# FoX attention values: block transposes on VectorE and fp32 products on eight 32x64 array tiles, with the values replicated through DRAM

## The chip, the cores and the metric

The kernel runs on one core of a Trainium2 chip. A core has TensorE (matrix products; the profile shows its products as PE and its weight loads as PEld), VectorE (DVE), ScalarE (ACT), GpSimd (POOL) and SyncE (SP), which here issues nearly all DMAs. Operands lie in SBUF, products arrive in PSUM (eight banks of 512 fp32 columns on 128 partitions). The metric is the device time of one execution in microseconds, as a median over runs. A profile comes from one execution of its own.

## The reference

One decoder layer for 1024 tokens of width 1024. An RMS norm and one input projection feed two groups of heads: eight HGRN2 heads (a gated linear recurrence) and sixteen FoX heads (softmax attention with a cumulative forget gate). Their gated outputs go through an output projection, a per-layer embedding gate and a final norm. What matters here is the FoX part, for a head of 64 features:

```python
for blk in range(S // Q):                      # Q = 128 queries
    q0, q1 = blk * Q, (blk + 1) * Q
    logits = einsum('bhtd,bhsd->bhts', qb, kb) * scale + F[..., q0:q1, None] - F[..., None, :q1]
    probs = softmax(where(mask, logits, -inf), axis=-1)
    outs.append(einsum('bhts,bhsd->bhtd', probs, vb))
```

So a block of 128 queries sees all earlier keys, and within its own 128 keys a triangle. All is fp32.

## The kernel before

The work goes in four stages: the start (norm, embeddings), the HGRN heads, the FoX heads, and the output projection with the gate and the final norm. Everything is kept feature-major, and fp32 accuracy is reached in the dense products by splitting both operands into exact float32r parts, hi and lo: three products (L363 in the helper `product_steps`) make one. A dense column tile (128 output features, 1024 tokens) is 48 such products of 512 columns.

The dense projections are not a stage of their own. The class `Ahead` holds them as jobs, generators that issue one product per step, and `ahead.fill(columns)` puts about so many columns of dense work between the steps of the heads. The tables `HGRN_FILL` and `FOX_FILL` give the amounts; `ahead.until(mark)` forces jobs until a tile is done; `ahead.flush()` issues what was put off in `ahead.pending`. `ahead.weights()` hands over a weight tile and starts the load of the next, in the order listed in `w_in_loads`. TensorE's instructions are pinned to program order by `pe`; the other engines follow the order that the scheduler finds.

The sixteen FoX heads go in eight pairs p (a pair fills 128 partitions), head i of a pair, and two chunks c of 512 queries, c = 1 first. A `Chunk` runs:

- `biases` and `diagonals`: loads the head's cumulative gate for all partitions, and GpSimd adds the causal bias for the four diagonal blocks.
- `softmax(b)` for a block of 128 queries, n = 128 (b + 1) keys: logits on TensorE in one or two pieces of up to 512 columns (L816 with the hi part of the keys, L817 with the lo part), on VectorE a fused add and minimum per piece (L820) and the minimum over the pieces (L826), on ScalarE the exponential with its sum (L827). The queries lie on the partitions.
- `transposed(j)`: TensorE transposes the 128x128 blocks of keys j for the chunk's query blocks (L835), ScalarE rounds the result out of PSUM into the float32r hi part (L844), VectorE subtracts for the lo part (L845). For the last key block of a chunk only half of a 256-column tile is live; its other half is zero (`last`, L838 and L839).
- `mix(following)`: over the key blocks j of the chunk, the two products of values with the hi and lo parts of the probabilities (L867, L868), accumulated in one PSUM bank. A value tile holds hi and lo of V side by side in its 128 columns, so the two halves of the result are added at the end (L873, L874). Between them go the softmaxes of the following chunk and the dense fills, and after j = 3 the flush.
- `norms`: the reciprocal of the softmax sums, transposed and passed through DRAM (`zd`, L887 and L888).

`fox_v(p)` makes the values: a dense tile, evacuated as `vt` (L480), transposed by four TensorE transposes per half (L485), and split into hi and lo in `vs` (L490, L491). PSUM in this stage: two banks for dense products, three for logits (`lg`), two for transposes (`tr`), one for the output (`av`).

In a pair, the jobs of the next pair are appended in the order q, k, gate of this pair (only pairs 1 to 5), v. The last chunk of a pair is preceded by `ahead.until(("k", p + 1))`. At the end, eight y tiles of the HGRN half are read back (`y_load`) into buffers of the FoX stage as these come free, four before pair 7 and four before the last chunk.

Of the kernel before, what the change touches and what calls it, by code (L numbers as in the profile page):

```python
# [33 lines left out]
FOX_FILL = (  # L34
    (1660, 3670, 8820, 2130, 2400),
    (3650, 8080, 7350, 2840, 3200),
    (3650, 8080, 7350, 2840, 3200),
    (3650, 8080, 7350, 2840, 3200),
    (3650, 8080, 7350, 2840, 3200),
    (3650, 8080, 7350, 2840, 3200),  # L40
    (2320, 5140, 6980, 2420, 2720),
    (1830, 4040, 7350, 1280, 1440),
)

# column tiles of w_in (128 columns each)
# [3 lines left out]
def shape_constants():  # L49
    """Identity, causal bias and block masks: functions of the shapes alone."""  # L50
# [3 lines left out]
    # keys (rows, within blocks of 32) that the columns of a block's three score groups keep  # L54
# [15 lines left out]
def trunk(ctx: ExitStack, tc: tile.TileContext, a, out):  # L70
# [12 lines left out]
    zd = dram.tile([16, S], F32, name="zd")  # L83

# [5 lines left out]
    def load_w(src, k, lo_engine=None, pin=lambda ins: ins):  # L90
        """One 128-column weight tile as exact float32r parts [P, k, P]."""
# [7 lines left out]
    def product(ps, terms, pin=lambda ins: ins):  # L99
        """ps = sum over terms of (stationary hi, lo) x (moving hi, lo), lo x lo left to rounding."""  # L100
# [6 lines left out]
    def dense(src, mov, evac, k=KT, lo_engine=None, w=None):  # L107
        """Feature-major projection of one column tile: evac(chunk, psum [P, CH])."""
# [7 lines left out]
    def add_squares(acc, sq, with_eps=False, pin=lambda ins: ins):  # L116
        """acc += sq; EPS enters the sum over the partitions once, so that ps / D below is mean + EPS."""
# [5 lines left out]
    def rstd(y, t, ps, pin=lambda ins: ins):  # L123
        """y = (ps / D) ** -0.5: the table's value and one Newton step."""
# [11 lines left out]
    def load_pair(tile0):  # L136
        """Two column tiles of w_in side by side, [P, k, 256], as float32r parts."""
# [8 lines left out]
    def token_major(w, v, blocks, evac_pin=lambda ins: ins):  # L146
        """Two column tiles with the tokens on partitions, [P, 2, block, 128]."""
# [6 lines left out]
    with ExitStack() as st:  # L154
# [3 lines left out]
        pin = tc.keep_in_program_order  # this section's engines run in the order below  # L158
# [36 lines left out]
        # per-layer embedding (halved), a [128, 512] piece at a time  # L195
# [118 lines left out]
        # HGRN lower bound: softmax over the single layer, cumulative sum minus the first  # L314
# [11 lines left out]
    class Ahead:  # L326
        """Dense products that fill the tensor engine's waits; weights are loaded a tile ahead."""
# [19 lines left out]
        def fill(self, columns=None):  # L347
            """Run jobs for about so many columns of moving operands, or all of them."""
# [27 lines left out]
    def w_in_loads():  # L376
# [4 lines left out]
        for p in range(PAIRS_F - 1):  # L381
            tiles += [T_FQ + p + 1, T_FK + p + 1] + ([T_FG + p] if 0 < p < PAIRS_F - 2 else []) + [T_FV + p + 1]
# [385 lines left out]
    with fox as st:  # L768
# [7 lines left out]
        for i in range(2):  # L776
            t = [fp.tile([P, 2 * P], F32R, name=f"last{i}{j}", bufs=1) for j in range(2)]
            for x in t:
                zeros(x[:, :P])
            last.append(t)  # L780

        class Chunk:
# [65 lines left out]
            def mix(self, following):  # L848
# [9 lines left out]
                for j in range(nj):  # L858
                    ph, pl, c0 = nxt
                    if j + 1 < nj:  # L860
                        nxt = self.transposed(j + 1)
# [265 lines left out]
```

## Time and profile before

| | |
|---|---|
| median of 3 runs | 1362.83 us (1361.51 to 1363.41) |
| span of the profiled execution, first to last instruction | 1361.6 us |
| mean granted TensorE clock | 0.993 |
| instructions | 22260 |
| FoX stage, from the first probability transpose to the last product with values | 563.9 to 1082 us |
| HBM read, written | 82.59 MB, 16.91 MB |

The profile names instructions by line, engine, operation and tiles, output left of the arrow. A group's line gives its count, then its busy time in us and the mean duration of one in ns, then the idle time of its engine just before it and what ended that. Durations of TensorE products overlap: a product's record lasts until its modelled end, while the next has long begun, so the distance between starts is what one costs in a stream. In the timeline a row starts with its start time and duration in us; consecutive instructions of one kind are merged, with a count. A row of the table by stage gives the stretch, its length, then busy us and instruction count for PE, PEld, DVE, ACT and POOL, then the granted clock (1.00 is full), the DMA engines' share and GB/s.

### The profile page before, as it was taken

To read this page: it belongs to the slowest core of one execution; us is meant where nothing else is said; L and a number is where in the kernel's file an instruction comes from. 1 tells how busy PE (TensorE), PEld (TensorE's weight loads), DVE (VectorE), ACT (ScalarE), POOL (GpSimd) and SP (SyncE) were. 2 spreads that over 40 slices of the span, in tenths; PEclk is the share of its full clock that TensorE was granted. 3 is DMA by queue.
4 is the path that set the end of the run, shared out by engine and by line. 5 is a ranking of instruction groups with operands and counts; after the bars stand their busy time and mean duration, and the time that the engine had idled before them with its cause. 6 is when DMAs were issued, how large, how long until landed. Compare 5 with 4: busy or idle time off the path is not lost.

```text
span 1361.6 us, 22260 instructions
## 1 busy us (share of the span) xinstructions
PE 1324.1 (97%) x8756; PEld 1116.9 (82%) x8756; DVE 802.6 (59%) x1976; ACT 552.6 (41%) x1128; POOL 373.7 (27%) x352
## 2 busy tenths in 40 slices
PE   6899999999999999999999999999999999999996
PEld 4787888888888878888888888888888888888895
DVE  6746575656746576576566666666666843333465
ACT  5413122221312233565555555555565711222455
POOL 3613123112211122344333333333342210101232
PEclk9999999999999999999999999999999999999998
DMA  7411111101101012112121112111123163212312
GB/s 282 144 45 63 48 38 58 63 17 63 48 32 63 19 47 80 47 56 70 55 71 55 56 55 70 54 55 55 70 84 118 63 240 108 85 47 70 132 63 78
DMA packets 35080, 100.93 MB, mean 74 GB/s; under 512 B 5008, under 2 KB 7312, under 8 KB 34976
## 3 DMA queue, kind: packets, MB, share of 16 engines
q1 hardware_dynamic: 34832, 98.99, 20.8%
q8 instruction: 69, 1.13, 0.3%
q0 software_dynamic: 144, 0.52, 0.1%
q14 instruction: 35, 0.29, 0.1%
HBM read 82.59 MB, written 16.91 MB: 73 GB/s over the span
## 4 chain that ended last, share of the span: by engine, by line
PE 87%; DVE 7%; ACT 4%; issue 1%; DMA 1%; SPq 0%; POOL 0%; DVEq 0%; ACTq 0%; POOLq 0%
PE ps L363 47%; PE pt L835 5%; PE ps L105 5%; PE ps L103 5%; PE ps L104 4%; PE po L868 3%; PE po L867 3%; PE lg L816 2%; PE lg L817 2%; PE ps L569 1%; PE gps L105 1%; PE gps L104 1%; PE gps L103 1%; DVE x L279 1%; PE po L712 1%
## 5 line engine op out<-in xcount | busy, mean ns | idle before, releaser
L363 PE MATMUL ps<-uhi,whi 128*128 128x512 f32 x896 | 355.9, 397 | 0.3 <-DVE q L451 0.3
L363 PE MATMUL ps<-ulo,whi 128*128 128x512 f32 x896 | 355.5, 397 | 0.0
L363 PE MATMUL ps<-uhi,wlo 128*128 128x512 f32 x896 | 354.6, 396 | 0.0
L88 POOL TENSOR_TENSOR wlo<-wf,whi 128x1024 fp32r<-128x1024 f32 x59 | 145.3, 2463 | 377.4 <-ACT whi L87 370.8
L363 PEld LDWEIGHTS ps<-uhi,whi 128*128 128x128 f32 x896 | 168.4, 188 | 31.5 <-PE ps L363 0.7
L363 PEld LDWEIGHTS ps<-ulo,whi 128*128 128x128 f32 x896 | 168.5, 188 | 30.4
L363 PEld LDWEIGHTS ps<-uhi,wlo 128*128 128x128 f32 x896 | 168.5, 188 | 30.4
L87 ACT CAST whi<-wf 128x1024 fp32r<-128x1024 f32 (+1 forms) x77 | 79.8, 1038 | 168.7 <-PE ps L104 90.4
L827 ACT ACTIVATE pr<-pr,mx 128x1024 f32<-128x1024 f32 (+7 forms) x128 | 99.6, 778 | 101.3 <-DVE mx L826 94.8
L845 DVE TENSOR_TENSOR pl<-pt,ph 128x512 fp32r<-128x512 f32 (+2 forms) x160 | 94.7, 607 | 75.9 <-ACT ph L844 74.6
L801 POOL TENSOR_TENSOR fm<-fbc,cst 128x128 f32<-128x128 f32 x128 | 59.0, 462 | 251.1 <-DVE mx L826 129.4
L844 ACT CAST ph<-pt 128x512 fp32r<-128x512 f32 (+2 forms) x160 | 79.8, 520 | 70.7 <-PE pt L835 60.1
L105 PE MATMUL ps<-yhi,wlo 128*128 128x512 f32 x256 | 99.6, 389 | 0.0
L103 PE MATMUL ps<-yhi,whi 128*128 128x512 f32 x256 | 99.6, 389 | 0.0
L104 PE MATMUL ps<-ylo,whi 128*128 128x512 f32 x256 | 99.6, 389 | 0.0
L820 DVE CUSTOM_DVE_ANT_0 pr<-lg,fbc 128x512 f32<-128x512 f32 (+3 forms) x176 | 82.0, 490 | 15.5 <-PE lg L817 15.2
L835 PE MATMUL pt<-cst,pr 128*128 128x128 f32 x576 | 89.3, 272 | 1.1 <-ACT pr L827 0.9
L835 PEld LDWEIGHTS pt<-cst,pr 128*128 128x128 f32 x576 | 71.4, 140 | 19.6 <-ACT pr L827 2.2
L816 PE MATMUL lg<-kh,q 128*128 128x512 f32 x192 | 74.7, 389 | 0.0
L817 PE MATMUL lg<-kl,q 128*128 128x512 f32 x192 | 64.1, 341 | 0.0
L867 PE MATMUL po<-ph,vs 128*128 128x512 f32 (+2 forms) x160 | 57.8, 361 | 0.1
L868 PE MATMUL po<-pl,vs 128*128 128x512 f32 (+2 forms) x160 | 57.9, 362 | 0.0
(214 smaller groups left out, 2498.3 us busy)
## 6 DMA issues: line engine op xcount, KB each, us to landing
wf<-in_w_in_dram SPq DMA_DIRECT2D x64, 512.0 KB
fbc<-fd SPq DMA_DIRECT2D x16, 512.0 KB
yf<-yd SPq DMA_DIRECT2D x16, 512.0 KB
wf<-in_w_out_dram SPq DMA_DIRECT2D x16, 512.0 KB
x<-in_xT_dram SPq DMA_DIRECT2D x8, 512.0 KB
pled<-pleo SPq DMA_DIRECT2D x16, 256.0 KB
xr<-in_xT_dram SPq DMA_DIRECT2D x16, 256.0 KB
yd<-sg SPq DMA_DIRECT2D x8, 512.0 KB
```

What stands on the lines that cost most here:

```text
L88: pin(lo_engine.tensor_tensor(out=lo, in0=src, in1=hi, op=ALU.subtract))
L103: pin(mm(ps, whi, uhi, start=i == 0, stop=False))
L104: pin(mm(ps, whi, ulo, start=False, stop=False))
L105: pin(mm(ps, wlo, uhi, start=False, stop=i == n - 1))
L363: pe(mm(ps, x, y, start=i == j == 0, stop=i == n - 1 and j == 2))
L816: pe(mm(ps[:, :w], tq, kh[:, s0 : s0 + w], start=True, stop=False))
L817: pe(mm(ps[:, :w], tq, kl[:, s0 : s0 + w], start=False, stop=True))
L827: nc.scalar.activation(pr, pr, AF.Exp, bias=mx[:, 0:1], scale=-1.0, accum_out=zs[:, b : b + 1])
L835: pe(nc.tensor.transpose(pt[:, b * P : (b + 1) * P], self.probs[b][:, j * P : (j + 1) * P], ident))
L845: nc.vector.tensor_tensor(out=pl, in0=pt[:, c0:], in1=ph, op=ALU.subtract)
L867: pe(mm(po[:, c0:], vs[:, j], ph, start=j == 0, stop=False))
L868: pe(mm(po[:, c0:], vs[:, j], pl, start=False, stop=j == nj - 1))
```

## The change

The probabilities are no longer transposed on TensorE. After the exponential, VectorE transposes the whole block row in one instruction, in blocks of 32x32: within each group of 32 partitions (queries 32 a to 32 a + 31 of the block) the result has keys on the partitions and queries along the free axis. The product with the values then contracts over 32 keys at a time, in fp32 without a split, on tiles of 32 rows and 64 columns of the array: row group a belongs to the queries 32 a, and even and odd key groups s go to the two column halves, with one PSUM bank per row group. Since row group a needs the values of key group s on its own 32 partitions, the values are needed on all four groups of partitions. They are written to DRAM and read back four times.

```diff
-    (3650, 8080, 7350, 2840, 3200),
+    (6500, 6500, 3300, 5700),
...
-            tiles += [T_FQ + p + 1, T_FK + p + 1] + ([T_FG + p] if 0 < p < PAIRS_F - 2 else []) + [T_FV + p + 1]
+            tiles += [T_FV + p + 1, T_FQ + p + 1, T_FK + p + 1] + ([T_FG + p] if 0 < p < PAIRS_F - 2 else [])
...
-                pt = tr.tile([P, CH], F32, name="pt", tag="tr")
+                pt = lg.tile([P, CH], F32, name="pt", tag="lg")
...
-                    nc.scalar.copy(dst[:, :, hi], pv[:, :, hi])
-                    nc.vector.tensor_tensor(out=dst[:, :, lo], in0=pv[:, :, hi], in1=dst[:, :, hi], op=ALU.subtract)
+                vo = fp.tile([P, 4, P], F32, name="vo", tag="tmp", bufs=3)
+                nc.scalar.copy(vo.rearrange("p b d -> p (b d)"), pt)
+                nc.sync.dma_start(out=vd[p, c * CH : (c + 1) * CH, :].rearrange("(b t) d -> t b d", t=P), in_=vo)
...
+    def load_v(p, quarters):
+        for g in quarters:
+            t = v_t.setdefault(p, [None] * 4)[g] = fp.tile([P, 8, P], F32, name=f"vr{g}", bufs=1)
+            for i in range(4):
+                nc.sync.dma_start(
+                    out=t[32 * i : 32 * i + 32], in_=vd[p, 256 * g : 256 * g + 256, :].rearrange("(s k) d -> k s d", k=32)
+                )
...
-        lg = st.enter_context(tc.tile_pool(name="lg", bufs=3, space=PSUM, reuse_waits="tile"))
-        tr = st.enter_context(tc.tile_pool(name="tr", bufs=2, space=PSUM, reuse_waits="tile"))
+        lg = st.enter_context(tc.tile_pool(name="lg", bufs=2, space=PSUM, reuse_waits="tile"))
...
-                self.probs[b - 4 * self.c] = pr
-            def transposed(self, j):
...
+                nc.vector.transpose(self.probs[:, b % 4, :n], pr)
+            def values(self):
+                po = av.tile([P, 4, CH], F32, name="po")
+                todo = []
+                for s in range(16 * self.c + 16):
+                    j, sub = s // 4 - 4 * self.c, s % 4
+                    for a in range(4):
+                        first = max(j + (sub > a), 0) if s > 1 else 0
+                        if first < 4:
+                            todo.append((s, a, first))
+                ends = {(s % 2, a): (s, a) for s, a, _ in todo}
+                for s, a, first in todo:
+                    rows = slice(32 * a, 32 * a + 32)
+                    pe(
+                        mm(
+                            po[64 * (s % 2) : 64 * (s % 2) + 64, a, 32 * first : P],
+                            v_t[self.p][s // 8][rows, s % 8, half[self.i]],
+                            self.probs[rows, first:, 32 * s : 32 * s + 32],
+                            start=s < 2,
+                            stop=ends[s % 2, a] == (s, a),
+                        )
+                    )
+                return po
...
+                before, after = FOX_FILL[self.p][:2], FOX_FILL[self.p][2:]
                 if following:
                     following.diagonals()
+                ahead.fill(before[self.c])
+                ahead.flush()
+                po = self.values()
+                if self.i == 1 and self.p < PAIRS_F - 1:
+                    load_v(self.p + 1, (2, 3) if self.c else (0, 1))
...
+                if following:
+                    for b in reversed(range(4 * following.c, 4 * following.c + 4)):
+                        following.softmax(b)
+                        ahead.fill(after[following.c])
...
         ahead.until(("v", 0))
+        ahead.flush()
+        load_v(0, range(4))
...
-                    ahead.jobs += [fox_q(p + 1), fox_k(p + 1)]
+                    ahead.jobs += [fox_v(p + 1), fox_q(p + 1), fox_k(p + 1)]
                     if 0 < p < PAIRS_F - 2:
                         ahead.jobs.append(fox_gate(p))
-                    ahead.jobs.append(fox_v(p + 1))
```

So `mix` no longer interleaves key blocks with softmaxes. It fills, issues all of the chunk's products with values in one burst, and then runs the four softmaxes of the following chunk, each followed by a fill. The new `FOX_FILL` rows are (fill before the values of c = 0, of c = 1, fill after each softmax of c = 0, of c = 1): (5000, 5000, 2400, 4200) for pairs 0 and 6, (6500, 6500, 3300, 5700) for 1 to 5, (3500, 3500, 1600, 2800) for 7. The output `po` now takes four PSUM banks, logits two instead of three, and the separate transpose banks are gone; the V transposes and those of `norms` use the logit banks. The values of pair 0 are loaded just before its first chunk, those of the next pair after the bursts of the second head of a pair, as the quarters come free. The block transposes of a chunk go to a buffer of their own for each c, and `pr` has two buffers. `vt`, `vo` and `avt` share three buffers. Of the y tiles, three are loaded before pair 7 and five before the last chunk. `xr` of the output projection moves to another pool. Comments were dropped from the file.

More of the change, by code (lines that the diff above doesn't have):

```diff
@@ L34 @@
 FOX_FILL = (
[L35 to L42 removed]
+    (5000, 5000, 2400, 4200),
+    (6500, 6500, 3300, 5700),
+    (6500, 6500, 3300, 5700),
+    (6500, 6500, 3300, 5700),
+    (6500, 6500, 3300, 5700),
+    (6500, 6500, 3300, 5700),
+    (5000, 5000, 2400, 4200),
+    (3500, 3500, 1600, 2800),
 )
@@ L83, in trunk @@
     zd = dram.tile([16, S], F32, name="zd")
+    vd = dram.tile([PAIRS_F, S, P], F32, name="vd")
     def split(hi, lo, src, lo_engine, pin=lambda ins: ins):
@@ L769, in trunk @@
         fp = st.enter_context(tc.tile_pool(name="fp", bufs=2, reuse_waits="tile"))
-        lg = st.enter_context(tc.tile_pool(name="lg", bufs=3, space=PSUM, reuse_waits="tile"))
-        tr = st.enter_context(tc.tile_pool(name="tr", bufs=2, space=PSUM, reuse_waits="tile"))
+        lg = st.enter_context(tc.tile_pool(name="lg", bufs=2, space=PSUM, reuse_waits="tile"))
         av = st.enter_context(tc.tile_pool(name="av", bufs=1, space=PSUM, reuse_waits="tile"))
-        last = []
[L776 to L780, printed above, removed]
         class Chunk:
@@ L827, in softmax @@
                 nc.scalar.activation(pr, pr, AF.Exp, bias=mx[:, 0:1], scale=-1.0, accum_out=zs[:, b : b + 1])
-                self.probs[b - 4 * self.c] = pr
-            def transposed(self, j):
-                first = max(j - 4 * self.c, 0)
-                pt = tr.tile([P, CH], F32, name="pt", tag="tr")
-                for b in range(first, 4):
-                    pe(nc.tensor.transpose(pt[:, b * P : (b + 1) * P], self.probs[b][:, j * P : (j + 1) * P], ident))
-                if first == 3:
-                    ph, pl = last[self.i]
-                    nc.scalar.copy(ph[:, P:], pt[:, 3 * P :])
-                    nc.vector.tensor_tensor(out=pl[:, P:], in0=pt[:, 3 * P :], in1=ph[:, P:], op=ALU.subtract)
-                    return ph, pl, 2 * P
-                c0 = first * P
-                ph = fp.tile([P, CH - c0], F32R, name="ph", tag="ph", bufs=2)
-                pl = fp.tile([P, CH - c0], F32R, name="pl", tag="pl", bufs=2)
-                nc.scalar.copy(ph, pt[:, c0:])
-                nc.vector.tensor_tensor(out=pl, in0=pt[:, c0:], in1=ph, op=ALU.subtract)
-                return ph, pl, c0
+                nc.vector.transpose(self.probs[:, b % 4, :n], pr)
@@ L857, in mix @@
-                po = av.tile([P, CH], F32, name="po")
[L858 to L861, printed above, removed]
-                    if blocks and j % (nj // 4) == 0:
-                        following.softmax(blocks.pop(0))
-                    ahead.fill(FOX_FILL[self.p][3 + self.c])
-                    if j == 3:
-                        ahead.flush()
-                    pe(mm(po[:, c0:], vs[:, j], ph, start=j == 0, stop=False))
-                    pe(mm(po[:, c0:], vs[:, j], pl, start=False, stop=j == nj - 1))
+                ahead.fill(before[self.c])
@@ L871, in mix @@
                 o = y_t[self.p]
-                tmp = fp.tile([P, CH], F32, name="avt")
-                nc.scalar.copy(tmp[hi], po[lo])
-                nc.vector.tensor_tensor(out=o[hi, sl], in0=po[hi], in1=tmp[hi], op=ALU.add)
+                tmp = fp.tile([P, CH], F32, name="avt", tag="tmp", bufs=3)
+                nc.scalar.copy(tmp[hi].rearrange("p (a x) -> p a x", a=4), po[lo, :, :P])
+                nc.vector.tensor_tensor(
+                    out=o[hi, sl].rearrange("p (b a t) -> p b a t", b=4, a=4),
+                    in0=po[hi, :, :P].rearrange("p a (b t) -> p b a t", b=4),
+                    in1=tmp[hi].rearrange("p (a b t) -> p b a t", a=4, b=4),
+                    op=ALU.add,
+                )
+                if following:
+                    for b in reversed(range(4 * following.c, 4 * following.c + 4)):
+                        following.softmax(b)
+                        ahead.fill(after[following.c])
             def norms(self, rz):
```

25 lines of the change are left out of this document (8 added, 17 removed).

## The prediction

> **What bounds the kernel now.** I read the busy shares first, then the table by stage over the FoX part (from the first probability transpose at 563.9 us to the last FoX product at 1082), then the chain that ended last.
>
> ```profile
> PE 1324.1 (97%) x8756; PEld 1116.9 (82%) x8756; DVE 802.6 (59%) x1976; ACT 552.6 (41%) x1128; POOL 373.7 (27%) x352
> 623.00:977.20 354.20, 354.20 (x1850) 296.68 (x1849) 215.05 (x711) 192.74 (x410) 131.95 (x151) 1.00 0.17 60
> 1038.10:1082.00 43.90, 42.98 (x239) 35.58 (x240) 34.38 (x111) 31.06 (x71) 9.44 (x10) 1.00 0.28 93
> PE ps L363 47%; PE pt L835 5%; PE ps L105 5%; PE ps L103 5%; PE ps L104 4%; PE po L868 3%; PE po L867 3%; PE lg L816 2%; PE lg L817 2%; PE ps L569 1%; PE gps L105 1%; PE gps L104 1%; PE gps L103 1%; DVE x L279 1%; PE po L712 1%
> ```
>
> Pairs 1 to 5 (second row, 354.2 us, 70.8 each) have TensorE busy in every microsecond at clock 1.00, with VectorE at 61%. Even the last pair, short of dense work, loses 0.9 us. So in FoX an instruction taken off TensorE is time saved, unless a wait takes its place. The two groups that the change removes, L835 and L867/L868, are on the chain.
>
> **What goes.** Busy times overlap, so I price by distances between starts. The timeline of TensorE:
>
> ```profile
> 714.30 0.93 PE L835 MATMUL pt<-cst,pr 128*128 128x128 f32 x7
> 714.98 0.48 PE L816 MATMUL lg<-kh,q 128*128 128x512 f32 x1
> 715.29 0.40 PE L817 MATMUL lg<-kl,q 128*128 128x512 f32 x1
> ...
> 704.01 0.39 PE L867 MATMUL po<-ph,vs 128*128 128x512 f32 x1
> 704.24 0.40 PE L868 MATMUL po<-pl,vs 128*128 128x512 f32 x1
> ...
> 708.50 0.34 PE L867 MATMUL po<-ph,vs 128*128 128x384 f32 x1
> 708.67 0.34 PE L868 MATMUL po<-pl,vs 128*128 128x384 f32 x1
> ...
> 710.82 0.28 PE L867 MATMUL po<-ph,vs 128*128 128x256 f32 x1
> 710.94 0.28 PE L868 MATMUL po<-pl,vs 128*128 128x256 f32 x1
> ...
> L835 PE MATMUL pt<-cst,pr 128*128 128x128 f32 x576 | 89.3, 272 | 1.1 <-ACT pr L827 0.9
> L867 PE MATMUL po<-ph,vs 128*128 128x512 f32 (+2 forms) x160 | 57.8, 361 | 0.1
> L867 PE MATMUL po<-last,vs 128*128 128x256 f32 x32 | 9.3, 291 | 0.0
> ```
>
> A product of 512 columns takes 0.23 us, of 384 0.17, of 256 0.12. Seven transposes run from 714.30 to 715.06 (715.29 less the 0.23 of the L816 between), 0.109 each: 576 x 0.109 = 63 us. The values are two instructions (L867, L868) per key block: 96 of 512 columns, 32 of 384 and 64 of 256, so 2 x (22.1 + 5.4 + 7.7) = 70 us. **Removed: 133 us.** The V transposes (four per tile) stay.
>
> **What comes on TensorE.** By `values`, a chunk c = 1 has 122 products with 12,544 columns, c = 0 58 with 4,384; a head 180 and 16,928; sixteen heads 2,880 and 270,848. Each fp32 product is two instructions: L569 is called 768 times and has 1536. The nearest rows:
>
> ```profile
> 301.87 0.39 PE L710 MATMUL po<-v,st 128*128 128x128 f32 x2
> 302.09 0.39 PE L712 MATMUL po<-state,x 128*128 128x128 f32 x2
> ...
> 282.29 0.39 PE L363 MATMUL ps<-ulo,whi 128*128 128x512 f32 x1
> 282.61 0.89 PE L569 MATMUL ps<-x,k 128*32 128x48 f32 x64
> 283.42 0.50 PE L363 MATMUL ps<-uhi,wlo 128*128 128x512 f32 x1
> 283.76 0.40 PE L363 MATMUL ps<-uhi,whi 128*128 128x512 f32 x1
> ...
> L569 PE MATMUL ps<-x,k 128*32 128x48 f32 x1536 | 21.3, 208 | 4.0 <-DVE k L589 4.0
> L660 PE MATMUL pd<-x,k 128*64 128x64 f32 x128 | 9.2, 225 | 0.0
> ```
>
> Whole-array fp32 with 128 columns: 0.22 us for the two instructions, 0.110 each. L660 keeps to one column tile: 16 instructions per head in 1.15 us, (1.15 - 0.225)/15 = 62 ns apart. L569 cycles through four column tiles: 64 in 0.89 us, (0.89 - 0.208)/63 = 10.8 ns apart, where 48 columns alone would need 41. So column tiles do run side by side, and 10.8 ns per instruction is attainable. Around such a burst the dense stream loses some 0.3 us (282.29 to 283.76 is 1.47; two dense products and 64 x 10.8 ns explain 1.15). No row shows tiles of 32 rows.
>
> I take all eight tiles as concurrent. A round of eight products then lasts 0.22 us at 128 columns, and never less than 16 x 10.8 ns = 0.17 us; round by round that is 3.10 us for c = 1 and 1.35 for c = 0, 71 us over sixteen heads; 32 bursts x 0.3 us add 10. **Added: 81 us.** Ends: below, 58 us (270,848 x 2 x 0.86 ns / 8), with 0.2 us per burst 65. Above, row groups that exclude each other: only two column tiles together, 233 + 10 = 243 us. I stand near the low end because L569, the one tiled row, has nearly its full factor.
>
> **Probabilities on VectorE.** L845, L839 and L491 go, 128 block transposes come. VectorE's start distances:
>
> ```profile
> 1054.22 0.68 DVE L820 CUSTOM_DVE_ANT_0 pr<-lg,fbc 128x512 f32<-128x512 f32 x1
> ...
> 1054.82 0.55 DVE L820 CUSTOM_DVE_ANT_0 pr<-lg,fbc 128x384 f32<-128x384 f32 x1
> ...
> 1055.30 0.28 DVE L820 CUSTOM_DVE_ANT_0 pr<-lg,fm 128x128 f32<-128x128 f32 x1
> 1055.51 0.08 DVE L820 DVE_READ_ACCUMULATOR2_ANT mx<- 128x1 f32 x1
> ...
> 1059.65 0.15 DVE L826 TENSOR_TENSOR mx<-mx 128x1 f32<-128x1 f32 x1
> L845 DVE TENSOR_TENSOR pl<-pt,ph 128x512 fp32r<-128x512 f32 (+2 forms) x160 | 94.7, 607 | 75.9 <-ACT ph L844 74.6
> L553 DVE TENSOR_SCALAR k<-k,oml 128x1024 f32<-128x1024 f32 x8 | 20.6, 2580 | 18.5 <-ACT k L540 18.5
> L554 DVE TENSOR_SCALAR f<-k 128x1024 f32<-128x1024 f32 x8 | 5.6, 694 | 0.3
> L827 ACT ACTIVATE pr<-pr,mx 128x640 f32<-128x640 f32 x16 | 13.3, 831 | 10.5 <-DVE mx L826 10.5
> ```
>
> 512, 384 and 128 columns cost 0.60, 0.48 and 0.21: about 1.02 ns per column and 0.08. At that price a c = 1 chunk (3,328 columns) pays 3.7 us and a c = 0 chunk (1,280) 1.6; 85 us in all against 95 for L845 alone, so VectorE's sum falls. Ends: 0.7 ns (L554) and 2.5 ns (L553) per column; I take the line through the L820 rows, which have the shapes and the stage.
>
> What matters is when the last transpose of a chunk ends, since the new values are one burst behind all four blocks. Behind the waiting products stand, in TensorE's fixed order, the next logits and all dense work. Four softmax reductions of c = 1 take VectorE from 1054.22 to 1059.73, less 0.53 of L845 and L839 between: 5.0 us. With 3.7 for transposes, 0.6 for the previous output and 1.8 of q/k/gate evacuation: 11.1 us. TensorE meanwhile does 3.0 us of logits and, in pairs 1 to 5, 4 x 5700 + 6500 columns at 0.45 ns, 13.2 us: covered. Not covered are these:
> - `until(("k", p+1))` pulls q, k and now also v (moved ahead of them) before the last chunk of a pair. Pairs 0 and 6 have no gate job, so the softmaxes that follow have no filler: 10.2 us of VectorE chain against 3.0 + 2.9 and 3.0 + 1.6 of TensorE, waits of 4.3 and 5.6.
> - In pairs 1 to 5 the last filler runs short: 0.5 us each.
> - Pair 7's fillers are 2800: logits end at 6.8 us, values could start at 9.6, the chain (reductions, 0.83 of exp, transpose) ends at 11.6, later where y splits come between: 3.5. Elsewhere 1.
>
> **Waits: 17 us**, ends 6 and 50 (transposes at 2.5 ns, nearly every c = 1 chunk late).
>
> At nothing I cost: ScalarE's copies (L844 goes, one V copy per tile comes; it only gets freer), the zero fills, the moved `xr`, and two logit buffers instead of three: the next logits come 2.6 us of filler after a block's reductions began, which end 1.5 us after it by the rows above. Where the filler is missing this is in the 10.2 us.
>
> **V through DRAM.** Pair 0 writes, then reads back before its first burst.
>
> ```profile
> 1006.13 0.28 SPq L887 DMA_DIRECT2D zd<-zt  x1
> 1007.35 0.45 SPq L888 DMA_DIRECT2D rz<-zd  x1
> ...
> 1083.77 0.45 SPq L888 DMA_DIRECT2D rz<-zd  x1
> ...
> 1087.52 2.46 POOL L895 TENSOR_TENSOR o<-o,rz 128x1024 f32<-128x1024 f32 x1 [22.97 <-DMA rz<-zd]
> ...
> GB/s 282 144 45 63 48 38 58 63 17 63 48 32 63 19 47 80 47 56 70 55 71 55 56 55 70 54 55 55 70 84 118 63 240 108 85 47 70 132 63 78
> ```
>
> A small write is done 1.2 us after issue, a 256 KB load 3.75. Evacuation, transposes, copy and write: about 5.7 us after the last V product. Sixteen loads, 2 MB at some 250 GB/s: 2 + 8 us more; values would end near 16.3, without DMA at 6.1 (2.2 of filler included). **Exposed 11**, ends 7 and 20 (runs of 512 bytes, of which the trace has no bulk load). Later pairs load after a burst and use it 16 us on; SyncE's queue waits there for that burst, and the weight loads behind it have a tile's 11 us. Five y loads instead of four wait for the last logits: **3** (0 to 8).
>
> **Sum.** Span 1361.6, runs 1362.8 in the median, so 1.2 around the span. -133 + 81 + 17 + 11 + 3 = -21: **1342 us** (likeliest case alone: 1318 to 1368).
>
> **Rivals.**
> 1. Row groups exclude each other, so the eight tiles work two at a time. For: no row has 32-row tiles, and four row groups must write PSUM at once. Against: column tiles overlap fully. 243 instead of 81 on TensorE; the longer bursts give VectorE time, waits fall to 3: -133 + 243 + 3 + 11 + 3, **1490, slower**. With such waits the change loses from an added cost of 116. Chance 0.08. The Trainium skill, page "TensorE: Matmul & The Clock Gate", section "Measured speedup vs the span model", has 3.07x for four row tiles and 10.6x for sixteen tiles; half of the latter would make the bursts 465 / 5.3 = 88 us instead of 71, and the sum 1359 (an estimate by that page). No run here shows it yet.
> 2. Weight loads are not hidden. Each product has its own load; one of 64 columns takes at most the 62 ns between L660's starts, and if 55 of them stood in line on the tile, half a product's 110, a round would take 1.5 times as long: 107 + 10 = 117, waits 15: **1376, slower**. It decides from 102 us added. For: two column tiles share each row group. Against: four share all rows in L569 and run at 10.8 ns. Chance 0.14. The same page, section "The mechanism", says that loads overlap running products only when the row group differs; by L569 the trace disagrees for column tiles.
> 3. VectorE or the V loads: transposes at the dear end, or exp waited for in VectorE's order, or late loads in each pair: waits of 50 in place of 17, 1375. Against: VectorE has 39% idle in the middle pairs. Chance 0.10.
> 4. Costs use the gain up to within 0.2% (what a measurement of this kernel can tell from no change): 0.03.
>
> **Chances.** Forecast 0.65 (0.60 faster, 0.03 same, 0.02 slower); rivals 2 and 3 reach down below 1360 in their milder forms, 0.05 faster and 0.01 same. Faster 0.65, same 0.07, slower 0.28. Range for 8 in 10: from 1312 (-133 + 65 + 10 + 7) to 1400 (-133 + 117 + 30 + 20 + 3, rival 2 with a mild rival 3 and the slow load); it leaves out rival 1 and the tails.
>
> **What would show it.** TensorE busy 70.8 to 65 us per middle pair; value bursts of 3.4 and 1.7 us, instructions 13 ns apart; a transpose of 1024 near 1.1 us; one gap near 564 us ended by a V load, two ended by VectorE after pairs 0 and 6. Bursts of 14 us would mean rival 1, of 5 rival 2, gaps before every c = 1 burst rival 3.

## The result, and the profile after

The changed kernel takes 1419.7 us in the median (1418.38 to 1422.17), against 1362.8 in runs beside it: a ratio of 1.0426, with a 95% interval of 1.0411 to 1.0441. It is slower by 57 us where 21 us of gain were forecast, and it lies outside the range. The profiled execution has a span of 1420.4 us, 58.8 more than before.

The page of the kernel after, busy shares first, then three groups (count, busy us, mean ns, then the idle time before them and what ended it):

```profile
PE 1315.5 (93%) x13556; PEld 1098.5 (77%) x13556; DVE 793.4 (56%) x1876; ACT 469.2 (33%) x920; POOL 370.5 (26%) x352
...
L846 PE MATMUL po<-pt,vr 32*64 32x128 f32 (+3 forms) x5760 | 96.8, 269 | 39.8 <-DVE pt L828 22.8 <-issue 14.7 <-DMA vr<-vd 1.8
...
L828 DVE STREAM_TRANSPOSE pt<-pr 128x128 f32<-128x128 f32 (+7 forms) x128 | 96.9, 771 | 25.5 <-ACT pr L827 24.3
...
L826 DVE TENSOR_TENSOR mx<-mx 128x1 f32<-128x1 f32 x176 | 59.7, 339 | 2.3
```

TensorE fell from 97% to 93% busy. L846 is the new product with values, L828 the new block transpose. Idle time in front of L846, with three different releasers, is new; before, almost nothing stood idle in FoX. The table by stage says how much. First the kernel before (FoX, then all that follows it), then the kernel after (FoX from the first to the last product with values, two of its pairs, and the rest):

```profile
563.96:1082.00 518.04, 516.85 (x2731) 432.66 (x2730) 332.13 (x1099) 296.13 (x637) 185.39 (x217) 1.00 0.19 66
1082.00:1361.60 279.60, 266.48 (x1350) 227.14 (x1349) 125.68 (x167) 90.34 (x138) 45.93 (x29) 0.98 0.29 101
```

```profile
564.50:1129.40 564.90, 498.94 (x7515) 408.73 (x7514) 316.72 (x995) 207.36 (x421) 182.95 (x216) 0.95 0.36 98
641.58:713.83 72.25, 65.51 (x971) 54.39 (x971) 40.87 (x130) 28.20 (x56) 25.86 (x30) 1.00 0.33 88
787.30:865.67 78.37, 70.75 (x971) 58.86 (x971) 41.22 (x130) 28.31 (x56) 26.32 (x31) 0.92 0.32 90
1129.40:1420.40 291.00, 276.16 (x1373) 234.22 (x1373) 131.66 (x173) 95.91 (x147) 45.29 (x29) 0.97 0.29 98
```

FoX is 46.9 us longer, what follows it 11.4, what leads up to it 0.5. In FoX three numbers of each row make the sum. TensorE is idle for 564.90 - 498.94 = 66.0 us (before: 1.2). Its mean clock is 0.95: the granted clock is 0.5 in 60.4 us of the stage (before: in none), and TensorE is busy for 50.5 us of these, so half clock costs about half of that, 25 us. What is left, 498.9 - 25 = 474 us of work at full clock, is 43 less than the 516.9 of before. So the change did take some 43 us off TensorE in FoX, where 52 were forecast (133 removed, 81 added), and lost twice that in two ways: TensorE waits, and it runs at half clock. Pair 1 (641.58) has all its 6.7 us of idle time at full clock, and its 65.51 us of work are the 65 us that the forecast gave a middle pair; pair 3 (787.30) has 7.6 us of idle time and a clock of 0.92 as well. The 11.4 us behind FoX are partly moved work: 20 dense products, 4.6 us of the 43, now come after the last burst.

What TensorE waited for in FoX (releaser, us in all, how often, the longest):

```profile
PE po L846 <- DVE pt L828: 22.8, 8, 5.1
PE po L846 <- issue: 14.7, 9, 3.3
PE lg L816 <- DVE mx L820: 6.5, 3, 2.7
PE lg L816 <- POOL kh L469: 3.8, 2, 2.0
PE lg L816 <- ACT vo L488: 3.4, 2, 1.7
...
PE ps L364 <- issue: 2.1, 2, 1.3
...
PE po L846 <- DMA vr<-vd: 1.8, 7, 0.3
...
PE lg L817 <- issue: 1.3, 1, 1.3
```

All rows of this view add up to 65.1 us. Two kinds are large: eight waits for the last transpose of a chunk, and twelve waits ("issue", 18.1 us in three rows) in which TensorE waited for nothing that the profile shows as a semaphore.

**The bursts themselves.** Timeline of TensorE, a c = 1 burst and a c = 0 burst that met no wait:

```profile
677.21 3.50 PE L846 MATMUL po<-pt,vr 32*64 32x128 f32 x244
680.63 0.50 PE L816 MATMUL lg<-kh,q 128*128 128x512 f32 x1
...
766.30 1.71 PE L846 MATMUL po<-pt,vr 32*64 32x128 f32 x116
767.94 0.50 PE L816 MATMUL lg<-kh,q 128*128 128x512 f32 x1
```

3.42 and 1.64 us from start to the next instruction, 14 ns per matmul. Sixteen heads make 16 x 5.06 = 81 us. The forecast had 71 for the bursts alone and 10 for their ends; the ends cost some 0.2 us per burst (the dense product before a burst and the one behind it take 0.32 and 0.34 us instead of 0.23), so like with like it is 87 against 81. At the forecast's 0.86 ns per column, the 12,544 columns of a c = 1 chunk would take 21.6 us one tile after another, and half of that two at a time. In 3.42 us, 6.3 tiles are at work in the mean, and their loads are hidden.

**The end of a pair.** TensorE, then VectorE, then GpSimd at the end of pair 2:

```profile
782.28 0.39 PE L364 MATMUL ps<-uhi,whi 128*128 128x512 f32 x1
787.30 6.20 PE L846 MATMUL po<-pt,vr 32*64 32x128 f32 x244 [4.63 <-DVE pt L828]
```

```profile
775.37 2.20 DVE L826 TENSOR_TENSOR mx<-mx 128x1 f32<-128x1 f32 x1
...
782.64 2.05 DVE L826 TENSOR_TENSOR mx<-mx 128x1 f32<-128x1 f32 x1
...
786.40 0.84 DVE L828 STREAM_TRANSPOSE pt<-pr 128x640 f32<-128x640 f32 x1 [1.05 <-ACT pr L827]
```

```profile
775.16 2.39 POOL L901 TENSOR_TENSOR o<-o,rz 128x1024 f32<-128x1024 f32 x1 [5.65 <-DMA vr<-vd]
...
782.33 2.34 POOL L89 TENSOR_TENSOR wlo<-wf,whi 128x1024 fp32r<-128x1024 f32 x1 [3.19 <-ACT whi L88]
```

The dense work of the pair ran out at 782.28 plus 0.23, and the burst waited until the transpose that began at 786.40 was done. Two minima of one column per partition took 2.20 and 2.05 us instead of 0.15. They end at 777.57 and 784.69; GpSimd's two operations end at 777.55 and 784.67. So VectorE's two-input instruction stood until GpSimd's was through, twice in one chain. It is no chance: of the 176 minima 55 last longer than 250 ns, and every one of these ends within 0.02 us of the end of a GpSimd operation (3 of the 121 short ones do). The Trainium skill, page "SBUF — State Buffer", section "SBUF: two separate sides", says that a VectorE operation with two SBUF inputs and a GpSimd operation that reads SBUF lock each other out for a whole instruction; the trace agrees to 0.02 us. The 6.20 us of the burst, instead of 3.5, is half clock.

**The supply of instructions.** TensorE in pair 3, and the instruction queue's transfers between 827.9 and 829:

```profile
824.25 2.89 PE L846 MATMUL po<-pt,vr 32*64 32x128 f32 x203
830.40 0.89 PE L846 MATMUL po<-pt,vr 32*64 32x32 f32 x33 [3.26 <-issue]
```

```profile
q8 instruction: 1, 0.02, 5.5%
```

This burst began at 824.09, just before the first row, and stops after 211 of its 244 matmuls; one 16 KB transfer of instructions runs from 827.97 to 828.93, and the burst goes on at 830.40. All twelve issue waits of FoX have this form: each ends 1.26 to 1.60 us after the end of a 16 KB transfer on the instruction queue. Eight stand in c = 1 bursts, after 166 to 237 matmuls, three just behind one, and one in the last c = 0 burst, after 99. A c = 1 burst is 244 matmuls and 244 loads in 3.4 us; the dense stream needs 55 us for as many instructions. The Trainium skill, page "Runtime: NRT & Kernel Launch", section "Instruction fetch mechanics", has blocks of 16 KiB for 256 instructions and calls the cost mostly hidden; the size agrees here, and the cost is not hidden in a burst of 488.

**The clock.** TensorE around the first burst:

```profile
560.03 0.80 PE L486 MATMUL pt<-cst,vt 128*128 128x128 f32 x4 [1.85 <-ACT vt L481]
...
561.48 0.63 PE L364 MATMUL ps<-uhi,wlo 128*128 128x512 f32 x1
561.90 0.63 PE L364 MATMUL ps<-uhi,whi 128*128 128x512 f32 x1
...
563.94 0.40 PE L364 MATMUL ps<-uhi,wlo 128*128 128x512 f32 x1
564.18 0.39 PE L364 MATMUL ps<-uhi,whi 128*128 128x512 f32 x1
...
564.50 1.86 PE L846 MATMUL po<-pt,vr 32*64 32x128 f32 x68
566.60 0.43 PE L846 MATMUL po<-pt,vr 32*64 32x128 f32 x2 [0.25 <-DMA vr<-vd]
...
573.23 0.50 PE L816 MATMUL lg<-kh,q 128*128 128x512 f32 x1
```

Behind a wait of 1.85 us the products come 0.42 us apart until about 563.8, then 0.24. The trace shows the granted clock at 0.5 for 3.4 us, or a multiple, at fourteen places between 535 and 1135 us, 68 us in all; before, there was none there. Not every wait does this. Of the six waits of 1.7 to 1.9 us around FoX, four had a half-clock stretch begin within 0.7 us behind them, and two (those that ended at 979.92 and 1039.79) had none; of the ten waits of 2 us or more, nine lay in one or had one begin during them or within 0.3 us behind them. The last rows also show pair 0's V: its first burst follows the loads from 564.50 to 573.23, 8.7 us instead of 3.4.

### The profile page after: what moved, and what is told of

It is laid out like the page before. It is cut to its first block, busy times and chain, and to the rows that moved or that the text cites. A ratio compares the mean times of both kernels' runs of the same rounds, so it can differ in the third digit from the quotient of the medians.

```text
span 1420.4 us, 31821 instructions
## 1 busy us (share of the span) xinstructions
PE 1315.5 (93%) x13556; PEld 1098.5 (77%) x13556; DVE 793.4 (56%) x1876; ACT 469.2 (33%) x920; POOL 370.5 (26%) x352
## 4 chain that ended last, share of the span: by engine, by line
PE 73%; DVE 14%; ACT 6%; issue 5%; DMA 1%; SPq 1%; POOL 0%; DVEq 0%; ACTq 0%; POOLq 0%
PE ps L364 39%; PE po L846 6%; PE ps L106 4%; PE ps L105 4%; PE ps L104 4%; DVE pt L828 3%; PE lg L816 2%; PE lg L817 2%; DVE mx L826 2%; DVE pr L820 2%; ACT pr L827 2%; PE ps L576 1%; PE gps L105 1%; PE gps L104 1%; PE gps L106 1%
## 5 line engine op out<-in xcount | busy, mean ns | idle before, releaser
L364 PEld LDWEIGHTS ps<-ulo,whi 128*128 128x128 f32 x896 | 171.9, 192 | 35.9 <-issue 1.2
L364 PEld LDWEIGHTS ps<-uhi,whi 128*128 128x128 f32 x896 | 171.5, 191 | 35.4 <-issue 1.5
L820 DVE CUSTOM_DVE_ANT_0 pr<-lg,fbc 128x512 f32<-128x512 f32 (+3 forms) x176 | 84.8, 488 | 173.7 <-PE lg L817 167.8
L827 ACT ACTIVATE pr<-pr,mx 128x128 f32<-128x128 f32 (+7 forms) x128 | 99.1, 775 | 166.5 <-DVE mx L826 163.7
L846 PE MATMUL po<-pt,vr 32*64 32x128 f32 (+3 forms) x5760 | 96.8, 269 | 39.8 <-DVE pt L828 22.8
L846 PEld LDWEIGHTS po<-pt,vr 32*64 32x64 f32 x5760 | 89.6, 139 | 54.0 <-DVE pt L828 27.2
L828 DVE STREAM_TRANSPOSE pt<-pr 128x128 f32<-128x128 f32 (+7 forms) x128 | 96.9, 771 | 25.5 <-ACT pr L827 24.3
L817 PE MATMUL lg<-kl,q 128*128 128x512 f32 x192 | 69.1, 364 | 1.4 <-issue 1.3
L816 PEld LDWEIGHTS lg<-kh,q 128*128 128x128 f32 x192 | 37.9, 197 | 31.5 <-DVE mx L820 8.0
L826 DVE TENSOR_TENSOR mx<-mx 128x1 f32<-128x1 f32 x176 | 59.7, 339 | 2.3
L105 PEld LDWEIGHTS ps<-ylo,whi 128*128 128x128 f32 x256 | 48.3, 189 | 12.4 <-DVE ylo L89 2.5
```

The source lines that it names most:

```text
L105: pin(mm(ps, whi, ulo, start=False, stop=False))
L364: pe(mm(ps, x, y, start=i == j == 0, stop=i == n - 1 and j == 2))
L816: pe(mm(ps[:, :w], tq, kh[:, s0 : s0 + w], start=True, stop=False))
L817: pe(mm(ps[:, :w], tq, kl[:, s0 : s0 + w], start=False, stop=True))
L820: nc.vector.tensor_tensor_reduce(out=pr[:, e0:e1], in0=ps[:, e0 - s0 : e1 - s0], in1=bias, scale=1.0, scalar=BIG, op0=ALU.add, op1=ALU.min ...
L826: nc.vector.tensor_tensor(out=mx[:, 0:1], in0=mx[:, 0:1], in1=mx[:, j : j + 1], op=ALU.min)
```

## The experiments

Losses of the forecast's kind (a wait) and two that it did not have (supply, clock) had to be told apart. The theory: VectorE's chain at a pair's end is late because GpSimd holds its minima and because the dense work there has run out; c = 1 bursts outrun the supply of instructions; a wait also brings half clock. Rivals: V through DRAM, the block transposes themselves, or the tiled products as such. The table has the medians, and for FoX (first to last product with values) TensorE's waits in us and its mean clock:

| kernel | us | ratio to before (95%) | for transposes | before logits | issue | clock |
|---|---|---|---|---|---|---|
| after | 1419.7 | 1.0426 (1.0411 to 1.0441) | 22.8 | 16.0 | 18.1 | 0.95 |
| e1_min | 1402.2 | 1.0295 (1.0278 to 1.0311) | 5.3 | 16.1 | 24.7 | 0.95 |
| e2_split | 1424.0 | 1.0442 (1.0423 to 1.0462) | 26.8 | 23.8 | 0.0 | 0.95 |
| e3_v_once | 1421.7 | 1.0431 (1.0406 to 1.0455) | 24.0 | 15.6 | 15.1 | 0.95 |
| e4_dummy | 1429.4 | 1.0493 (1.0464 to 1.0521) | 10.8 | 15.9 | 23.0 | 0.96 |
| e5_fill | 1410.4 | 1.0350 (1.0322 to 1.0379) | 2.4 | 25.2 | 21.6 | 0.96 |
| e6_all | 1401.1 | 1.0292 (1.0277 to 1.0308) | 2.6 | 21.0 | 3.3 | 0.97 |
| e7_ahead | 1393.4 | 1.0232 (1.0210 to 1.0254) | 3.4 | 16.6 | 3.5 | 0.99 |
| e8_before_min | 1362.6 | 1.0002 (0.9993 to 1.0011) | | | | |
| e9_cut | 1390.6 | 1.0211 (1.0194 to 1.0228) | 12.5 | 16.7 | 4.2 | 0.97 |
| e10_one_cut | 1382.4 | 1.0143 (1.0123 to 1.0164) | 7.9 | 12.8 | 3.2 | 0.98 |
| e11_v_first | 1375.8 | 1.0099 (1.0084 to 1.0115) | 6.8 | 14.9 | 4.0 | 0.98 |
| e12_cover | 1370.1 | 1.0066 (1.0048 to 1.0084) | 2.8 | 16.2 | 4.2 | 0.99 |

The waits before logits stay at 13 to 25 us in every version; the kernel before has none. In nine of the twelve kernels the larger part is for L820, VectorE's reading of a logit bank, and the kernels with the change have two such banks where the kernel before has three. No run gives the third bank back, so it is not shown how much of these waits comes from the missing bank and how much from VectorE being late.

### The minima

```diff
-                                in1=bias, scale=1.0, scalar=BIG,
+                                in1=bias, scale=1.0, scalar=mx[:, parts - 1 : parts] if parts else BIG,
...
-                for j in range(1, parts):
-                    nc.vector.tensor_tensor(out=mx[:, 0:1], in0=mx[:, 0:1], in1=mx[:, j : j + 1], op=ALU.min)
-                nc.scalar.activation(pr, pr, AF.Exp, bias=mx[:, 0:1],
+                nc.scalar.activation(pr, pr, AF.Exp, bias=mx[:, parts - 1 : parts],
```

> The 176 minima of 128x1 (L826) are gone: each partial reduction starts from the minimum of the one before. Theory (the values of a pair's last c = 1 chunk come late because VectorE's chain of four softmax blocks is late, and that chain is held by minima which wait some 2 us for GpSimd's two-input instructions): TensorE's waits for the transposes fall from 22.8 us to 8-12, the half-clock stretches behind them from 17 in all to 10-12, the time to 1392-1406. Rival (the block transposes themselves, 97 us of VectorE, or the loads of V are the bound): no more than the minima's own 26 us of an idle engine go, 1415-1420.

1402.2, 17.5 us less than after, inside the theory's interval (the waits for transposes fell further than expected, to 5.3 instead of 8 to 12). Two rows of what TensorE waited for in FoX:

```profile
PE po L844 <- issue: 22.7, 12, 3.1
...
PE po L844 <- DVE pt L826: 5.3, 7, 1.4
```

Waits for the transposes fell by 17.5 us. That it is the same number as the time is partly chance: all waits in FoX fell by 13.9, and TensorE's busy time by 3.9. The transposes are as long as before the edit (775 ns in the mean against 771), so their length did not make the chain late. The mean clock stayed at 0.95, which the theory did not expect, while issue waits grew by 6.6. The same edit in the kernel before:

> The kernel before, with only the minima folded into the reductions. Theory (there TensorE has work in every microsecond of FoX, so VectorE's chain is covered and GpSimd's hold on it costs nothing): within 2 us of before, 1361-1364. Rival (the minima cost time in both kernels): 1345-1357.

1362.6, a ratio of 1.0002. Before, GpSimd held the minima too (51 of 176 last longer than 250 ns, each to within 0.02 us of the end of a GpSimd operation), as one row of VectorE's groups of that kernel shows:

```profile
L826 DVE TENSOR_TENSOR mx<-mx 128x1 f32<-128x1 f32 x176 | 51.6, 293 | 3.2
```

A mean of 293 ns for an instruction that takes 150 alone. There dense work covered it: behind this chain TensorE waited 0.9 us in all of FoX. The change took that cover away at the pairs' ends.

### The cover at a pair's end

```diff
-                        ahead.fill(after[following.c])
+                        ahead.fill(after[following.c] if following.p == self.p else 4100)
```

> Only the fill behind each softmax block of a pair's last stage changes, from 5700 (4200) columns to 4100, so that in pairs 1 to 5 some 12 more dense products are left between the last logits and the value burst; pairs 0 and 6 have no dense work there in either kernel. Theory (the wait before the burst is VectorE's late chain less the dense work that is left): each of the five ends gains 1 to 2.5 us of cover, waits for the transposes 22.8 to 10-15 us, the time 1405-1415. Rival (the chain gets later with it, as the logits come no earlier): 1418-1423.

1410.4, as the theory had it. The rows:

```profile
PE lg L816 <- DVE mx L820: 15.2, 8, 2.9
...
PE po L846 <- DVE pt L828: 2.4, 5, 0.8
```

The waits for transposes almost vanish, more than expected, but less dense work stands between the logits now, and of the 20 us, 8.7 come back there as waits for the reductions. The cover is one quantity that can be spent once.

### The supply of instructions

```diff
-                for s, a, first in todo:
+                for k, (s, a, first) in enumerate(todo):
+                    if self.c and k in (30, 61, 92):
+                        ahead.fill(IN_BURST)
```

> The c = 1 bursts are cut in four by three fills of 2048 columns (4 dense products each), which are taken from later fills. Theory (the stalls of 0.5 to 3.3 us in and behind c = 1 bursts, some 18 us in all, are a supply of instructions that a burst of 488 loads and matmuls in 3.5 us outruns): stalls fall under 4 us, and the half clock behind them with it, 1398-1408. Rival (the stalls are a cost of the tiled products, or of the loads that run beside them): the sum of the stalls stays within 3 us, 1416-1423.

1424.0: the waits went as the theory had it, and the time did not; the interval overlaps that of after. No issue wait is left (18.1 to 0.0), so it is not the tiled products or their loads, only their number in a row. But the three fills per burst ask for 12,288 columns per pair on top of the other fills, with no more dense work to give, so the pairs' ends ran out sooner:

```profile
PE po L849 <- DVE pt L829: 26.8, 14, 4.6
PE lg L817 <- DVE mx L821: 18.8, 8, 2.9
```

With the demand kept the same, and one cut of 4096 columns in the middle of the burst (`k == 61`), on top of the folded minima:

> Minima folded, and each c = 1 burst cut once, in its middle, by 4096 columns of dense work (2560 in pair 7) that are taken from the fills before and behind it, so that the demand on the pair's dense work stays the same. Theory (a burst of 488 instructions outruns the supply, one of 244 does not): the 24.7 us of issue stalls of the kernel with the minima folded go under 5, and with them part of its half clock; 16 more cuts at some 0.3 us are paid; 1378-1392 against its 1402. Rival (the stalls belong to the tiled products whatever their number in a row, or cutting costs as much as it saves): 1397-1406.

1390.6 against 1402.2: issue waits from 24.7 to 4.2, the clock from 0.95 to 0.97, while the waits for transposes rose by 7.2; less dense work stands before the burst there, which would explain it. Supply is shown as a cause of its own, worth some 20 us of waits in these kernels and, net of the other waits, some 11 us of time here.

### V through DRAM

```diff
-                            v_t[self.p][s // 8][rows, s % 8, half[self.i]],
+                            v_t[0][s // 8][rows, s % 8, half[self.i]],
...
-                if self.i == 1 and self.p < PAIRS_F - 1:
-                    load_v(self.p + 1, (2, 3) if self.c else (0, 1))
```

> The V of pairs 1 to 7 is projected, transposed and written, but not read back: all pairs use the V of pair 0 in the value products (the output changes). Theory (only pair 0 waits for V; later loads have 16 us): 1414-1420, a few tenths of us per pair at most. Rival (14 MB of reads in runs of 512 bytes slow the weight loads, SyncE's queue or TensorE's operands): 1380-1400, waits and half clock shrink in pairs 1 to 5.

1421.7; the interval overlaps that of after. Reading 14 MB less changes nothing: the rival falls. Pair 0 is tried further below.

### The clock

In each fill at a pair's end, when the jobs are used up, products into a PSUM tile that nobody reads:

```diff
+            for _ in range(9 if columns > 4200 else 5):
+                pe(mm(ps, u[0][0][:, :P], u[0][0][:, :CH], start=True, stop=True))
```

> 85 products of 512 columns that nobody reads (19.3 us of TensorE at full clock) are added where the fill of a pair's last stage runs out: 9 in each of pairs 1 to 5, 4 x 5 in pairs 0 and 6. Theory (a wait also halves the clock for 3.4 to 6.8 us after it, so a wait of 4 us costs up to 7): waits for VectorE there shrink by what the products fill, fewer half-clock stretches, and the time falls although work is added, 1403-1414. Rival (the clock follows the bursts or costs nothing that matters): the products fit into the waits or push beyond them, 1418-1428.

1429.4, on the rival's side and 1.4 us above its interval. Of 19.3 us of added work, waits for transposes took up 12.0; the waits before logits stayed (16.0 and 15.9), and issue waits rose by 4.9. The clock went from 0.95 to 0.96 only. So filling waits with idle work does not pay, and this run does not show what half clock costs in all; the product spacing above shows it locally. That the clock follows the waits and not the bursts is seen along the table: it rises to 0.99 in kernels with the same number of tiled products and fewer waits, and it stays at 0.95 in e2_split, whose bursts are cut in four but whose waits for transposes and before logits are 50.6 us instead of 38.8.

### Three parts together

Folded minima, three fills of 2048 columns in each c = 1 burst, and a table that asks for less:

```diff
-    (6500, 6500, 3300, 5700),
+    (5500, 4500, 2300, 5300, 4600),
```

The fifth number is the fill behind the softmaxes at a pair's end.

> Three parts in one: minima folded into the reductions, c = 1 bursts cut in four by dense products, and a fill table with some 8000 columns less demand per pair, so that dense work remains at the pair's end. Theory (three separate causes: chain held by GpSimd, instruction supply, missing fill): issue stalls under 4 us, waits for transposes under 6, the losses in pairs 0 and 6 remain; 1365-1385. Rival (the causes share one limit, for instance TensorE's clock under the tiled products): about the 1402 of the kernel with the minima folded alone, 1395-1410.

1401.1, a miss: no better than the minima alone, though waits for transposes and for issue were nearly gone. Pairs 1 to 5 took 70.1 to 70.8 us. A cut in the burst, in the timeline of TensorE:

```profile
742.93 0.39 PE L365 MATMUL ps<-uhi,whi 128*128 128x512 f32 x1
743.25 1.17 PE L847 MATMUL po<-pt,vr 32*64 32x128 f32 x60
744.35 0.50 PE L365 MATMUL ps<-ulo,whi 128*128 128x512 f32 x1
744.69 0.40 PE L365 MATMUL ps<-uhi,wlo 128*128 128x512 f32 x1
```

The dense product before the tiles lasts 0.32 us instead of 0.23, the one behind them 0.34: 0.2 per cut, and the tiles' own end about 0.1 more. 48 cuts are some 14 us, and the waits before logits rose from 16.1 to 21.0; these two could account for the 16 us or more that were expected and did not come, but were not tried apart here.

### Dense work for pairs 0 and 6, and fewer cuts

```diff
-                    ahead.jobs += [fox_v(p + 1), fox_q(p + 1), fox_k(p + 1)]
-                    if 0 < p < PAIRS_F - 2:
-                        ahead.jobs.append(fox_gate(p))
+                    ahead.jobs += [fox_v(p + 1), fox_q(p + 1), fox_k(p + 1), fox_gate(p + 1)]
```

> As the kernel of three parts, and the gate projection of pair p + 1 is made at the end of pair p for all pairs (two gate buffers; a few small tiles get one buffer less), so that pairs 0 and 6 have dense work there too; pair 7 has less of it. Theory (pairs 0 and 6 lose 18 and 9 us to a stage without dense work and the half clock behind it): 10 to 25 us less than the kernel of three parts, 1345-1365; pair 7 gives some of it back. Rival (those pairs lose their time to the first loads of V and to the tail): within 5 us of it.

1393.4: 7.7 us less where the theory had 10 to 25, so a miss in size. The clock in FoX is 0.99 now, but pair 0 still takes 74.3 us, and pairs 1 to 5 take 70.7 to 72.5. Then one cut per burst, of 5120 columns, a fill table that asks for nearly all dense work, and the reciprocal's transpose in a list of its own:

```diff
-                    if self.c and k in (30, 61, 92):
+                    if self.c and k in (61,):
...
-            ahead.pending.append(transpose)
+            ahead.late.append(transpose)
```

> The kernel with gates a pair ahead, with one cut of 5120 columns per c = 1 burst in place of three of 2048, a fill table that asks for nearly all dense work of a pair, and V's transposes no longer flushed right behind the reciprocal's one. Theory (each entry into and exit from a burst costs TensorE 0.3 us together; the remaining waits for reductions and for V's evacuation are missing cover): 28 cuts fewer give 8, the evacuation 6, the cover some 5: 1370-1382 against 1393. Rival (something else, such as slower dense products beside the tiled ones, sets the pair's 72 us): 1388-1396.

1382.4, 11 us less, 0.4 above the theory's upper edge; pairs 1 to 5 went down to 68.5 to 69.3 us. Then V of pair 0 before its k:

```diff
-        ahead.jobs.append(fox_k(0))
+        ahead.jobs += [fox_v(0), fox_k(0)]
         ahead.until(("k", 0))
-        ahead.jobs.append(fox_v(0))
+        ahead.flush()
+        load_v(0, range(4))
+        ahead.jobs.append(fox_v(1))
```

> The same, and V of pair 0 is projected before its k and read back while k and the first logits run; V of pair 1 fills in its place. Theory (pair 0 still waits for its V: its first burst lasts 8 to 9 us instead of 3.5 as it follows the loads, and the clock halves behind it): the first burst lasts 3.5 to 4 us apart from its cut, 4 to 9 us less than the kernel without it. Rival (the loads were hidden by the cuts already, or pair 0 lacks the dense work that moved): within 3 us of it.

1375.8: 6.6 us less, as the theory had it. No wait for V is left in FoX; pair 0's exposed V had a price, 6.6 of the forecast's 11 us. Last, more cover at the pairs' ends (2500 columns; cuts of 4096 instead of 5120):

```diff
-                ahead.fill(before[self.c])
+                ahead.fill(before[self.c] + (2500 if 0 < self.p < PAIRS_F - 1 and self.i == 0 and self.c else 0))
```

> The kernel with V of pair 0 first, with 2500 columns more between a pair's last logits and the next pair's first burst in pairs 1 to 5 (they come from the next pair's V), some more between the blocks of c = 1, and cuts of 4096 columns in place of 5120. Theory (what is left at the pair ends is missing cover, 6.8 us of waits for transposes and 13.4 for reductions): waits for the transposes under 2 us, pairs 1 to 5 at 67.5 to 68.3 us instead of 68.5 to 69.9, the time 1364-1373. Rival (VectorE is the limit of a pair by now): 1374-1378.

1370.1, within the theory's interval (waits for transposes 2.8 where under 2 were expected). It is the best of the series, and still slower than before by 0.66% (0.48 to 0.84). Pairs 1 to 5, then pair 7 of this kernel:

```profile
635.80:976.70 340.90, 333.11 (x4851) 270.81 (x4850) 188.33 (x540) 142.56 (x280) 133.32 (x151) 1.00 0.39 102
1043.50:1089.50 46.00, 34.58 (x807) 26.08 (x807) 29.04 (x83) 20.24 (x44) 4.99 (x10) 0.93 0.26 90
```

340.9 / 5 = 68.2 us per pair, 2.7 less than the 70.9 of before: with cover, the change gains in the middle pairs. TensorE is idle for 11.4 us of pair 7's 46; two of its dense tiles were given to earlier pairs. No version tried beats the kernel before.

## Why the prediction was wrong

- **Removed 133, added 81.** Right but for 6 us. The bursts take 81 us where 71 were worked out, their ends 6 where 10 were allowed: 87 in place of 81. The stage's work at full clock fell by 43 where 52 were forecast; with 87 added that makes some 130 removed, close to the 133, which no run measures by itself. **Rival 1** (1490, bursts of 14 us) and **rival 2** (1376, bursts of 5 us) fall with the bursts of 3.42 us. The rates of the Trainium skill, page "TensorE: Matmul & The Clock Gate", section "Measured speedup vs the span model", would have made the bursts 88, without their ends (an estimate by that page); the trace has 81.
- **Transposes on VectorE.** Right in size: 97 us busy where 85 were forecast; one of 1024 columns takes 1.24 by its record and 1.17 from start to start, where 1.1 was forecast.
- **Waits of 17 us (6 to 50).** This step failed. In FoX the waits for engines (not issue, not V) are 65.1 - 18.1 - 1.8 = 45 us, inside its upper end, but at other places than named. It named unfilled stages behind pairs 0 and 6, which came at their size (5.3 and 5.5 us where 4.3 and 5.6 were forecast), and gave pairs 1 to 5 0.5 us each; these waited 3.1 to 5.1 at their ends, 20.7 us together in place of 2.5. Two inputs were wrong. The chain was priced at 11.1 us, with a minimum of 0.15 us from one row, while the group's mean in the kernel before was 293 ns; at the end of pair 2 it took 19.3 us (from the end of the burst before, 767.94, to that of the last transpose), of which GpSimd's two holds are 4.0 and the rest mostly waits for logits and exponentials. And the cover was taken as 13.2 us of dense work in each c = 1 stage, while `until(("k", p + 1))` and the fills before it leave only the 48 products of a gate for the last stage of a pair, of which two stood behind the last logits, with 13 of the next pair's V. **Rival 3** (1375) was nearest: VectorE late, waits of 50. Its cause was another, and it was still 45 us too low, as it too had only waits.
- **Issue, not in the sum.** 18 us. The forecast took the price of an instruction from bursts of 128 (64 matmuls with their loads) and did not ask whether 488 in a row can be supplied.
- **Half clock, not in the sum.** Some 25 us in FoX. A wait was priced at its length. In the kernel before, half clock showed only before 64 us and behind 1350 us, where the mean clock of 0.993 comes from.
- **V of pair 0: 11 us.** Right, though not as one gap: the wait of 1.85 us for V's evacuation, 5.3 us of stretched burst, and two half-clock stretches (3.4 us lost) make 10.5. Later pairs at nothing: right, by e3_v_once.
- **The end: 3 us (0 to 8).** 11.4, of which 4.6 are dense products that moved behind the last burst; the rest are half clock and waits for y's splits, not tried apart.

The sum by what was found: -43 of work in FoX, +65 of idle time net of before, +25 of clock, +11 behind it, +0.5 ahead: +58.8. So the step that failed is the one that turns freed TensorE work into time: waits were 45 us at engines instead of 17, and the 18 us of supply and 25 of half clock had no term. What was hidden before, a chain that GpSimd holds, became the bound at the pairs' ends as soon as the dense work there ran out, and TensorE's own losses came on top. How much of the half clock would go with each wait is open, as no run takes it away alone.

## What to carry to other kernels

Before taking work off an engine that is never idle, count, in its program order, what is left to issue between the last producer and the waiting consumer, and price the chain with group means, not with the shortest row: a small two-input VectorE instruction whose mean is twice its shortest was here being held by GpSimd. Do not put hundreds of short matmuls with a load each in a row without asking for their supply: here one cut, which left some 250 instructions on each side, took 20 of 25 us of waits, and each further cut cost 0.3 us. Price a TensorE wait of 2 us or more at its length and half a clock stretch of 3.4 us besides, as nine of ten such waits had one here.

## What the hardware showed that was not expected

- Tiled fp32 products of 32 rows and 64 columns on all eight tiles run at 14 ns per matmul, loads hidden, over 244 in a row (3.42 us).
- Such a stream, with a load for each matmul, stopped in eight of the sixteen c = 1 bursts, after 166 to 237 matmuls, and went on 1.26 to 1.60 us after the end of a 16 KB transfer of instructions; with eight dense products in the middle of the burst, issue waits fell from 24.7 to 4.2 us in FoX.
- Waits of 1.7 to 1.9 us were enough, in four cases of six, for a stretch of 3.4 us at half clock behind them (1.85 us before 560.03, 1.71 before 594.41), in which 512 columns take 0.43 us instead of 0.23.
- A VectorE minimum of one column took 2.05 and 2.20 us instead of 0.15, and ended within 0.02 us of GpSimd's two-input operation beside it.
